# A hybrid decoder layer on one core: the memory projection moved to the front, and the first two column tiles made an ordinary pair

## The chip, the cores and the metric

One core of a Trainium2 chip runs the whole program in one launch. The metric is device time in microseconds (us). The engines are TensorE (PE, with its weight loads as PEld), VectorE (DVE), ScalarE (ACT), GpSimd (POOL) and SyncE (SP), which issues the transfers between the chip's memory and the core.

## The reference, cut to what matters

One layer over 1,056 tokens (1,024 of a prompt and 32 of decoding) with 2,048 features, all in float32. Only group D, the memory attention, and the projections are touched by the change.

```
h    = rmsnorm(x, g_norm)                       # x: 1056 x 2048
proj = h @ w_in                                 # columns of groups A (conv), B (GLA), C (window), D (memory)
kv   = rmsnorm(mem, g_mem) @ w_mem_kv           # mem: 256 x 2048, kv: 256 x 1024
k, v = split(kv);  k = rmsnorm(k per head, g_mem_k)
q    = rmsnorm(m_q per head, g_mem_q)           # 4 heads of 128
o    = softmax(q k^T / sqrt(128)) v;  y_d = o * silu(m_z)
y    = x + concat(y_a, y_b, y_c, y_d) @ w_out
```

## The kernel before

Everything lies transposed: features on the partitions, tokens along the row. Each float32 operand of a large product is split into a rounded high part and the remainder (names ending in h and l), and three products (wh sh, wl sh, wh sl) stand for one.

**Pairs.** The projections go by pairs of column tiles (128 columns each), as a Strassen product with seven products per pair and phase. A phase is one half of the 2,048 features. `first_pair` runs the first half and keeps the sums in memory (`half_in`), `second_pair` adds the second half. One product (`product`, L668) is 24 matmuls of 128 x 264. The seven combinations of x (B11, T2, B21, T1, T3, B22, T4) stay in the on-chip memory for a whole phase. `make_weights` makes the weight side of a product (ACT rounds, L644; DVE takes the remainder, L645, and makes sums, L626 to L640). `ORDER` names the pairs: 22 of the input projection. The first phase runs all 22, then the second phase all 22 with the attention and the other groups beside them, then eight output pairs go through both phases.

**Start.** The tiles Dq0 and Dq1 (the queries of heads 0 and 1) are no pair. `first_two` multiplies them by x directly (L406, 288 matmuls of 128 x 352, both halves of the features), while `load_x` brings x tile by tile (k = 0 to 15), splits it (ACT L310, DVE L311), squares it (ACT L289) and adds the squares up (DVE L294). `row_norms` makes R, the scale of each token, along every partition. The result is scaled on its way out of PSUM (L415) to two tiles dq, which are held until their attention is done.

**First strands.** `first_strands` is a generator. It scales the first half of x by g_norm and R (L444, `normal`), makes the seven combinations (L470 to L482), splits each (`split`, ACT L429, DVE L430) and computes a small product for group B, `rank` (L498). `product` advances it when a combination is missing.

**Memory.** `memory` is a generator too: 16 steps, one per 128 features of the memory tokens, each with 12 matmuls of 128 x 512 (L902). It scales and splits the memory tokens (`prepare`, ACT L848, DVE L849), splits the weights (`weights`, ACT L881, DVE L882) and sums squares as a tree (`squares`, ACT L856, DVE L858). It advances with the strands inside the first pair. `memory_out` scales the keys and values.

**Heads.** `d_head` queues the attention of one head: a preparation and four units of 256 tokens (`d_unit`, L1007 scores, L1029 transposes, L1037 values). A pipe (`_Pipe`) starts queued work at two steps per product. Heads 0 and 1 are queued after the first pair of the first phase. Heads 2 and 3 follow the pair Dq2, Dq3 of the second phase, and behind them `d_decode` (its key and value loads kc and vc). A gate of group D then waits for it.

A scheduler places the instructions of each engine before the run; on an engine they run in that order. All transfers are issued by SP, in order, with eight semaphores in rotation: a load waits for the one eight before it. The pool `rt` has ten buffers of a full row of tokens (x tiles, squares, d, q, z, kc, vc), the pool `sp` fourteen of 2,112 columns.

Of the kernel before, what the change touches and what calls it, by code (L numbers as in the profile page):

```python
# [14 lines left out]
P = 128  # L15
# [6 lines left out]
NCH = 3  # L22
# [100 lines left out]
class _Step:  # L123
    def __init__(self, nc, tc, ctx, I, O):
# [19 lines left out]
        self.pieces, self.raw, self.ready, self.done = [], [], [], 0  # L144
        self.xh, self.xl = [None] * KT, [None] * KT
# [127 lines left out]
    def load_x(self):  # L273


        nc = self.nc
        self.acc = [None] * 2
        last = None
# [5 lines left out]
        self.x0, self.x0raw = block, raw  # L284

        def square(k, parts):
            sq = self.rtile("sq") if k < 8 else parts[2]
            for i, p in enumerate(parts[:2]):
                nc.scalar.activation(sq[:, i * H : i * H + H], p, AF.Square)  # L289
            i = int(k % 4 == 3)  # L290
            if self.acc[i] is None:
                self.acc[i] = sq
            else:
                nc.vector.tensor_tensor(self.acc[i], self.acc[i], sq, op=ALU.add)  # L294
        for k in range(KT):
            if k < 8:
                parts = [block(2 * (k // 4) + i, k % 4) for i in range(2)]
            else:
                xr = self.rtile("xr")
                parts = [xr[:, 0:H], xr[:, H:TOK], xr]  # L300
            if k < 8:
                for i in range(2):
                    nc.sync.dma_start(out=parts[i], in_=self.I["xT"][k, :, i * H : i * H + H])
            else:
                nc.sync.dma_start(out=parts[2], in_=self.I["xT"][k])
            hl = self.stile(F32R, "xhl")
            for i in range(2):
                h, l = (hl[:, x * TOK + i * H : x * TOK + i * H + H] for x in range(2))
                g = self.gn[:, k : k + 1]
                nc.scalar.activation(h, parts[i], AF.Copy, scale=g)  # L310
                nc.vector.scalar_tensor_tensor(l, parts[i], g, h.bitcast(F32), op0=ALU.mult,  # L311
                                               op1=ALU.subtract)
            self.xh[k], self.xl[k] = hl[:, 0:TOK], hl[:, TOK : 2 * TOK]
            if last:
                square(*last)
            last = k, parts
            if k == KT - 1:
                square(*last)
            yield k

    def row_norms(self, spare):

        nc = self.nc
        acc = self.acc[0]
        nc.vector.tensor_tensor(acc, acc, self.acc[1], op=ALU.add)
        for sums in self.token_sums(acc[:, 0:SEQ]):
            pass
        nc.tensor.matmul(spare[:, 0:2], acc[:, TOK - P : TOK], self.ones[:, 0:2], start=True,
                         stop=True)
        r = self.small(NB + 1, tag="rx")  # L330
        self.rsqrt(r[:, 0:NB], sums, 1.0 / D_MODEL, EPS, NB)
        self.rsqrt(r[:, NB : NB + 1], spare[:, 0:1], 1.0 / D_MODEL, EPS, 1)
        for g in range(3):
            ps = self.ps() if g == 1 else spare
            blocks = list(range(4 * g, min(4 * g + 4, NB + 1)))
            for i, n in enumerate(blocks):
                nc.tensor.transpose(ps[:, i * P : i * P + P],
                                    r[:, n : n + 1].to_broadcast([P, P]), self.ident)
            if g < 2:
                nc.scalar.copy(self.R[:, 512 * g : 512 * g + 512], ps)  # L340
            else:
                nc.scalar.copy(self.R[:, SEQ:TOK], ps[:, P - NS : P])

    def load_piece(self):
        kind, src = self.pieces[len(self.raw)]
        wr = self.wp.tile([P, 512], F32, name=self.name("wr"), tag="wr", bufs=6)
        self.nc.sync.dma_start(out=wr, in_=src)
        self.raw.append(wr)  # L350

    def split_piece(self):
        nc = self.nc
        n = len(self.ready)
        wr = self.raw[n]

        if n % 2:
            wh, wl = self.r5(), self.r5()
        else:
            wh, wl = self.weights()  # L360
        if n:
            nc.scalar.copy(wh, wr)
        else:
            nc.vector.tensor_copy(wh, wr)
        eng = nc.gpsimd if 0 < n < 8 else nc.vector
        eng.tensor_tensor(wl, wr, wh.bitcast(F32), op=ALU.subtract)
        self.ready.append((wh, wl))
# [4 lines left out]
    def take(self, ahead=2):  # L372
        p = self.done
        self.done += 1
        last = len(self.pieces) - 1
        while len(self.ready) <= min(p + ahead, last):
            while len(self.raw) <= min(len(self.ready) + 1, last):
                self.load_piece()
            self.split_piece()
        while len(self.raw) <= min(p + ahead + 1, last):  # L380
            self.load_piece()
        return self.ready[p]

    def first_two(self, evacs):

        nc = self.nc
        a, b = self.two(), self.two()
        ps = [[a[:, 0:512], a[:, 512:1024], b[:, 0:512]], [self.ps() for _ in range(NCH)]]
        self.load_piece()
        xs = self.load_x()  # L390
        next(xs)
        self.load_piece()
        for _ in range(3):
            next(xs)
        for kq in range(4):
            w = [self.take(1) for _ in range(2)]
            for kk in range(4):
                next(xs, None)
                k = 4 * kq + kk
                for i in range(2):  # L400
                    wh, wl = w[i]
                    ks = slice(kk * P, kk * P + P)
                    pairs = [(wh, self.xh[k]), (wl, self.xh[k]), (wh, self.xl[k])]
                    for c in range(NCH):
                        for n, (y, x) in enumerate(pairs):
                            nc.tensor.matmul(ps[i][c][:, 0:CW], y[:, ks],  # L406
                                             x[:, c * CW : c * CW + CW], start=(k == 0 and n == 0),
                                             stop=(k == KT - 1 and n == 2))
                if kq == 3 and kk == 1:
                    self.row_norms(b[:, 512:1024])  # L410
        for i in range(2):
            dst = evacs[i]
            for c in range(NCH):
                cs = slice(c * CW, c * CW + CW)
                nc.vector.tensor_tensor(dst[:, cs], ps[i][c][:, 0:CW], self.R[:, cs], op=ALU.mult)  # L415
# [16 lines left out]
    def first_strands(self):  # L432
# [7 lines left out]
        def normal(b):  # L440
            for k in range(4 * (b // 2), 4 * (b // 2) + 4):
                x = self.x0(b, k % 4)
                h = slice(H * (b % 2), H * (b % 2) + H)
                v.scalar_tensor_tensor(x, x, self.gn[:, k : k + 1], self.R[:, h], op0=ALU.mult,  # L444
                                       op1=ALU.mult)
# [6 lines left out]
        ps = self.two()  # L452
# [378 lines left out]

    def memory(self, pool):
# [6 lines left out]
        raw = [None] * KT  # L839
        parts = {}  # L840

        def prepare(k):
            mh, ml = self.r5(), self.r5()
            for i in range(2):
                m = raw[k // 8][:, (k % 8 + i) * N_MEM : (k % 8 + i + 1) * N_MEM]
# [7 lines left out]
        def squares(k):  # L853
            nonlocal acc
            t = raw[k][:, 0 : 8 * N_MEM]
# [8 lines left out]
        for k in range(2):  # L864
            raw[k] = self.stile(F32, "mr")
            nc.sync.dma_start(out=raw[k][:, 0 : 8 * N_MEM].rearrange("p (k t) -> p k t", k=8),
                              in_=I["memT"][8 * k : 8 * k + 8].rearrange("k p t -> p k t"))
        wraw, ready = {}, {}

        def load(k):  # L870
            if k < KT:
                wraw[k] = self.rtile("wm")
                nc.sync.dma_start(out=wraw[k][:, 0:1024], in_=I["w_mem"][k])

        def weights(k):
            w = wraw.pop(k)
            ready[k] = []
            for c in range(2):
                wh, wl = self.weights() if c else [self.t5().bitcast(F32R) for _ in range(2)]
                x = w[:, 512 * c : 512 * c + 512]  # L880
                nc.scalar.copy(wh, x)  # L881
                nc.vector.tensor_tensor(wl, x, wh.bitcast(F32), op=ALU.subtract)  # L882
                ready[k].append((wh, wl))
            load(k + 2)
# [1055 lines left out]
```

## Time and profile before

| | |
|---|---|
| time, median of 3 runs | 1568.07 us (1562.56 to 1576.54) |
| the profiled execution | 1575.27 us, span 1573.5 us |
| PE, PEld, DVE, ACT busy | 97%, 93%, 70%, 49% of the span |
| chain that ended last | PE 75%, DVE 13%, ACT 5%, DMA 4% |
| HBM read, written | 165.38 MB, 69.41 MB |

Times below are from the start of the span. A row of a group reads: line, engine, operation, out<-in, shapes, count | busy us, mean ns of one | idle time of the engine just before, and what ended it. A row of the timeline reads: start, length, engine, line, operation, count [idle before <- what ended it]. An xN on a timeline row is the number of records; a matmul on plain float32 leaves two records.

### The profile page before, as it was taken

What the parts mean: (1) busy time and instruction counts of PE and PEld (TensorE: products, weight loads), DVE (VectorE), ACT (ScalarE), POOL (GpSimd) and SP (SyncE); (2) the same over time, 40 slices, a digit from 0 to 9 for tenths busy, and PEclk for the clock granted to TensorE, in tenths of its full rate; (3) what the DMA queues carried; (4) which work ended last, traced back from release to release, by engine and by line L of the source; (5) the groups of instructions that cost most, each with busy time, mean ns of one, the idle gap of its engine ahead of it and who ended that gap; (6) DMA issues with size and microseconds to landing.
All of it is one profiled execution on the core that took longest, in us unless ns stands there. A gap on an engine that the chain in (4) does not pass through costs nothing.

```text
span 1573.5 us, 30753 instructions
## 1 busy us (share of the span) xinstructions
PE 1530.4 (97%) x12194; PEld 1459.6 (93%) x12194; DVE 1105.2 (70%) x2283; ACT 772.6 (49%) x1620; POOL 23.3 (1%) x35
## 2 busy tenths in 40 slices
PE   7889999999999999999999999999998999999998
PEld 7668999999999999988998999999988999999998
DVE  8998645586555559665767776967779777596664
ACT  8466633322333336744468774645557443363332
POOL 3000000000000000000000000000000000000000
PEclk9899999999999999999999999999999999999999
DMA  7523222375332248158423333533437224587651
GB/s 272 193 92 109 69 103 94 142 267 193 109 110 100 95 148 308 62 144 298 139 78 84 109 90 121 173 123 90 167 119 244 82 104 168 188 288 267 209 203 63
DMA packets 102418, 236.77 MB, mean 150 GB/s; under 512 B 16516, under 2 KB 22532, under 8 KB 102276
## 3 DMA queue, kind: packets, MB, share of 16 engines
q1 hardware_dynamic: 102276, 234.82, 44.4%
q8 instruction: 96, 1.57, 0.4%
q14 instruction: 46, 0.38, 0.1%
HBM read 165.38 MB, written 69.41 MB: 149 GB/s over the span
## 4 chain that ended last, share of the span: by engine, by line
PE 75%; DVE 13%; ACT 5%; DMA 4%; issue 3%; SPq 0%; DVEq 0%; ACTq 0%
PE pj L668 64%; PE ms L902 2%; DVE wl L645 2%; DMA sx<-xs 1%; DVE s L430 1%; DVE xhl L311 1%; ACT wh L644 1%; ACT t L1280 1%; PE ms L1037 1%; DMA x<-in_xT 1%; ACT xhl L310 1%; DMA kc<-in_cache_mem_kT 1%; DVE t L1267 1%; PE ms L1313 1%; PE ms L1007 1%
## 5 line engine op out<-in xcount | busy, mean ns | idle before, releaser
L668 PE MATMUL pj<-s,wh 128*128 128x264 f32 x6720 | 1268.7, 288 | 7.6 <-ACT pj L751 5.5
L668 PEld LDWEIGHTS pj<-s,wh 128*128 128x128 f32 x6720 | 1055.5, 189 | 25.6 <-issue 12.7
L668 PE MATMUL pj<-s,wl 128*128 128x264 f32 x3360 | 960.3, 286 | 0.8 <-DVE wl L645 0.8
L668 PEld LDWEIGHTS pj<-s,wl 128*128 128x128 f32 x3360 | 636.7, 190 | 5.9 <-issue 4.1
L644 ACT CAST wh<-wr 128x512 fp32r<-128x512 f32 x300 | 186.3, 621 | 262.4 <-PE pj L668 248.3
L645 DVE TENSOR_TENSOR wl<-wr,wh 128x512 fp32r<-128x512 f32 x300 | 206.5, 688 | 119.8 <-ACT wh L644 119.4
L698 DVE TENSOR_TENSOR d<-d,pj 128x528 f32<-128x528 f32 x180 | 121.4, 701 | 102.1 <-PE pj L668 60.0
L644 ACT CAST wh<-ws 128x512 fp32r<-128x512 f32 x120 | 74.5, 621 | 93.9 <-PE pj L668 89.5
L645 DVE TENSOR_TENSOR wl<-ws,wh 128x512 fp32r<-128x512 f32 x120 | 82.5, 688 | 9.1 <-ACT wh L644 8.5
L751 ACT COPY pj<-d 128x528 f32<-128x528 f32 x120 | 72.5, 604 | 15.1 <-DVE u L761 5.5
L430 DVE TENSOR_TENSOR s<-sx,s 128x1056 fp32r<-128x1056 f32 x42 | 51.6, 1250 | 1.9 <-ACT s L429 1.9
L429 ACT CAST s<-sx 128x1056 fp32r<-128x1056 f32 x42 | 44.3, 1075 | 10.0 <-DMA sx<-xs 5.2
L772 DVE TENSOR_TENSOR d<-d,pj 128x528 f32<-128x528 f32 x30 | 21.1, 703 | 36.5 <-PE pj L668 36.5
L701 ACT COPY d<-pj 128x528 f32<-128x528 f32 x30 | 18.0, 599 | 55.1 <-PE pj L668 55.1
L707 ACT COPY d<-pj 128x528 f32<-128x528 f32 x30 | 18.0, 601 | 53.4 <-PE pj L668 53.4
L1280 ACT ACTIVATE t<-t,sm,sm 128x256 f32<-128x256 f32 (+1 forms) x64 | 37.1, 581 | 14.2 <-DVE sm L1272 14.2
L640 DVE TENSOR_TENSOR wr<-wr,ws 128x512 f32<-128x512 f32 x60 | 41.8, 697 | 1.0
L775 DVE TENSOR_TENSOR d<-u,pj 128x528 f32<-128x528 f32 x30 | 21.1, 703 | 30.1 <-PE pj L668 30.0
L626 DVE TENSOR_TENSOR ws<-wr,wr 128x512 f32<-128x512 f32 x60 | 41.3, 688 | 1.2
L636 DVE TENSOR_TENSOR wr<-wr,wr 128x512 f32<-128x512 f32 x60 | 41.3, 688 | 1.1
L627 DVE TENSOR_TENSOR ws<-ws,wr 128x512 f32<-128x512 f32 x60 | 41.3, 688 | 1.0
L778 DVE TENSOR_TENSOR d<-u,pj 128x528 f32<-128x528 f32 x30 | 21.1, 703 | 29.8 <-PE pj L668 29.6
(368 smaller groups left out, 1524.2 us busy)
## 6 DMA issues: line engine op xcount, KB each, us to landing
wr<-in_w_in SPq DMA_DIRECT2D x184, 256.0 KB
half_in<-d SPq DMA_DIRECT2D x44, 528.0 KB
d<-half_in SPq DMA_DIRECT2D x44, 528.0 KB
sx<-xs SPq DMA_DIRECT2D x42, 528.0 KB
wr<-in_w_out SPq DMA_DIRECT2D x64, 256.0 KB
x<-in_xT SPq DMA_DIRECT2D x24, 528.0 KB
xs<-t SPq DMA_DIRECT2D x36, 264.0 KB
half_out<-d SPq DMA_DIRECT2D x16, 528.0 KB
```

The lines of the kernel that those rows point to most:

```text
L429: nc.scalar.copy(h[:, s], x)
L430: nc.vector.tensor_tensor(l[:, s], x, h[:, s].bitcast(F32), op=ALU.subtract)
L626: v.tensor_tensor(s1, r(1, 0), r(1, 1), op=ALU.add)
L627: v.tensor_tensor(s2, s1, r(0, 0), op=ALU.subtract)
L636: v.tensor_tensor(x, r(0, 0), x, op=ALU.subtract)
L640: v.tensor_tensor(x, x, self.wsum[n][1], op=ALU.subtract)
L644: nc.scalar.copy(wh, x)
L645: v.tensor_tensor(wl, x, wh.bitcast(F32), op=ALU.subtract)
L668: nc.tensor.matmul(ps[:, 512 * c : 512 * c + CG], w[:, ks], x[:, xs], start=(first and kk == 0 and n == 0), stop=(kk == 3 and n == 2), ski ...
L698: nc.vector.tensor_tensor(o, o, bank(ps), op=op)
L751: nc.scalar.copy(bank(ps), x)
L1280: nc.scalar.activation(ps[u][:, g, kts[0] : 2], ps[u][:, g, kts[0] : 2], AF.Exp, bias=mx[:, c : c + 1], scale=rq[:, 4 * m + c : 4 * m + c ...
```

## The change

1. `first_two`, `load_x` with its split of x, and the weight pieces for it are gone. Dq0 and Dq1 stand at the head of `ORDER`, so there are 23 pairs in each phase of the input projection.
2. A new `start` brings x (`load_x(k)`), the memory tokens (`load_mem`) and w_mem (`load_mem_weights`) interleaved. It advances `memory` by 8 steps, and by 3 more inside `row_norms`. ACT squares x. DVE multiplies the first eight tiles of x by g_norm in place. PE sums the squares over the partitions (`sum_squares`: four matmuls of 32 x 264 for each k, at four column positions of the array, into one bank of PSUM).
3. `normal` multiplies a block by R alone: one operation on 2,112 columns, or two on 1,056.
4. `memory` splits 1,024 columns of a weight tile in one operation of each engine, into a buffer of the pool `sp`.
5. All four heads are queued in the second phase, each two behind their pair.

```
+    def square(self, k):
+        nc = self.nc
+        if k < 8:
+            sq = self.sq[k] = self.rtile("sq")
+            for i in range(2):
+                x = self.x0(2 * (k // 4) + i, k % 4)
+                nc.scalar.activation(sq[:, i * H : i * H + H], x, AF.Square)
+                nc.vector.tensor_scalar(x, x, self.gn[:, k : k + 1], None, op0=ALU.mult)
+        else:
+            nc.scalar.activation(self.sq[k], self.sq[k], AF.Square)
+    def sum_squares(self, k):
+        for j in range(4):
+            self.nc.tensor.matmul(self.sums[32 * j : 32 * j + 32, 0:CG], self.ones[:, 0:32],
+                                  self.sq[k][:, CG * j : CG * j + CG], start=(k == 0),
+                                  stop=(k == KT - 1), tile_position=(0, 32 * j))
...
+        def loads(k):
+            if k in (1, 4, 7):
+                self.load_mem(k // 3 + 1)
+            if k + 2 < KT:
+                self.load_mem_weights(k + 2)
+            for i in range(2):
+                if 2 * k + i < KT:
+                    self.load_x(2 * k + i)
+        for k in range(2):
+            loads(k)
+        for k in range(8):
+            if k + 2 < 8:
+                loads(k + 2)
+            next(self.mem)
+            for i in range(2):
+                self.square(2 * k + i)
+            if k:
                 for i in range(2):
+                    self.sum_squares(2 * k - 2 + i)
+        self.load_weights(0, ((0, 0), (1, 0), (1, 1), (0, 1)))
+        self.make_weights()
         for i in range(2):
+            self.sum_squares(KT - 2 + i)
+        for _ in self.row_norms(spare):
+            next(self.mem)
...
         def normal(b):
-            for k in range(4 * (b // 2), 4 * (b // 2) + 4):
-                x = self.x0(b, k % 4)
-                h = slice(H * (b % 2), H * (b % 2) + H)
-                v.scalar_tensor_tensor(x, x, self.gn[:, k : k + 1], self.R[:, h], op0=ALU.mult,
-                                       op1=ALU.mult)
+            r = self.R[:, H * (b % 2) : H * (b % 2) + H].unsqueeze(1)
+            for x in self.x0raw[b] if b == 3 else [self.x0raw[b]]:
+                n = x.shape[1] // H
+                t = x.rearrange("p (k t) -> p k t", k=n)
+                v.tensor_tensor(t, t, r.to_broadcast([P, n, H]), op=ALU.mult)
...
-    ORDER = ["Dq2", "Dq3", "Ac0", "Ah0", "Az0", "Ab0", "Dz0", "Dz1", "Dz2", "Dz3",
+    ORDER = ["Dq0", "Dq1", "Dq2", "Dq3", "Ac0", "Ah0", "Az0", "Ab0", "Dz0", "Dz1", "Dz2", "Dz3",
...
                     if n == 0:
                         self.masks()
-                        for h in range(2):
-                            self.d_head(q[h], h)
                 pipe.drain()
                 done = [2]
-                self.second(hold(q))
-                for h in (2, 3):
-                    self.d_head(q[h], h)
+                for i in (0, 2):
+                    self.second(hold(q))
+                    for h in (i, i + 1):
+                        self.d_head(q[h], h)
```

Three places show how instructions move. The first is ACT in the changed kernel, some twenty operations into the program. Names: r is a scaled part of the memory tokens, wm the high half of a weight tile of memory, sq a tile of squares of x, xr an x tile of the second half that is squared in place (xr_240 is k = 8, sq_303 and sq_308 are k = 6 and 7).

```order
L827 ACTIVATE r_244<-mr_129,consts 128x256 x2
L850 CAST wm_250<-wr_134 128x1024
L850 CAST wm_288<-wr_146 128x1024
L297 ACTIVATE sq_265<-xb_125 128x528
L297 ACTIVATE sq_265<-xb_126 128x528
L297 ACTIVATE sq_270<-xb_125 128x528
L297 ACTIVATE sq_270<-xb_126 128x528
L300 ACTIVATE xr_240<-xr_240 128x1056
L827 ACTIVATE r_327<-mr_129,consts 128x256 x2
L300 ACTIVATE xr_242<-xr_242 128x1056
L297 ACTIVATE sq_303<-xb_125 128x528
L297 ACTIVATE sq_303<-xb_127 128x528
```

The square of k = 8 stands ahead of those of k = 6 and 7, though SP loads it behind them.

The second place is DVE where the first block of x is scaled by R; before the change it stood like this (dq: the direct product's result, xb_128: the first block of x, t and wl: low halves of memory's weights).

```order
L415 TENSOR_TENSOR dq_120<-ms_125,R_118 128x352
L444 SCALAR_TENSOR_TENSOR xb_128<-xb_128,consts,R_118 128x528 x4
L882 TENSOR_TENSOR t_747<-wm_736,t_746 128x512
L882 TENSOR_TENSOR wl_751<-wm_736,wh_750 128x512
L444 SCALAR_TENSOR_TENSOR xb_129<-xb_129,consts,R_118 128x528 x2
L430 TENSOR_TENSOR s_785<-xb_128,s_784 128x2112
L882 TENSOR_TENSOR t_763<-wm_738,t_762 128x512
```

In the changed kernel DVE has at the same place (sm: the small steps of the inverse root, mr: the tree of memory's squares, L410: the scaling, L395: the low half of a combination):

```order
L268 SCALAR_TENSOR_TENSOR sm_508<-sm_527,sm_508 8x4
L828 SCALAR_TENSOR_TENSOR r_622<-mr_236,consts,r_621 128x256 x2
L591 TENSOR_TENSOR ws_1110<-wr_466,wr_1007 128x512
L601 TENSOR_TENSOR wr_466<-wr_464,wr_466 128x512
L837 TENSOR_TENSOR mr_236<-mr_236 128x1024
L410 TENSOR_TENSOR xb_123<-xb_123,R_118 128x2112
L410 TENSOR_TENSOR xb_124<-xb_124,R_118 128x2112
L395 TENSOR_TENSOR s_618<-xb_123,s_617 128x2112
L851 TENSOR_TENSOR wm_627<-wr_432,wm_627 128x1024
L851 TENSOR_TENSOR wm_676<-wr_544,wm_676 128x1024
```

Thirteen of memory's sixteen weight tiles are split by then where none was, and the tree's first addition (L837) stands right ahead of the scaling.

The third place is PE in the changed kernel at the end of the start (pj_128 holds the sums of squares, then the transposes; ms_154 to ms_157 are memory's sums of which the first is shown).

```order
L306 MATMUL pj_128<-xr_360,ones 32x264 x4
L306 MATMUL pj_128<-xr_362,ones 32x264 x4
L873 MATMUL ms_154<-wm_429,r_391 128x512 x2
L873 MATMUL ms_154<-wm_429,r_392 128x512
L873 MATMUL ms_156<-wm_429,r_391 128x512 x2
L873 MATMUL ms_156<-wm_429,r_392 128x512
L873 MATMUL ms_155<-wm_429,r_391 128x512 x2
L873 MATMUL ms_155<-wm_429,r_392 128x512
L873 MATMUL ms_157<-wm_429,r_391 128x512 x2
L873 MATMUL ms_157<-wm_429,r_392 128x512
L320 MATMUL pj_128<-ident,t_480 128x128 x2
L322 MATMUL pj_128<-ident,t_480 8x128
```

One step of the memory product stands between the last sum of squares and the transposes of the sums.

More of the change, by code (lines that the diff above doesn't have):

```diff
@@ L295, in load_x @@
[L295 to L306, printed above, removed]
-            for i in range(2):
[L308 to L319, printed above, removed]
+        self.x0, self.x0raw, self.sq = block, raw, [None] * KT
@@ L326, in row_norms @@
[L326 to L342, printed above, removed]
@@ L346, in load_piece @@
[L346 to L367, printed above, removed]
+        rows = self.t5()[:, 0:CG]
@@ L369, in weights @@
+        yield
     def weights(self):
         return [self.wp.tile([P, 512], F32R, name=self.name(x), tag=x) for x in ("wh", "wl")]
[L372 to L399, printed above, removed]
-                for i in range(2):
[L401 to L410, printed above, removed]
+    def start(self, pool):
+        self.x_tiles()
+        self.mem_tiles = {}
+        self.mem = self.memory(pool)
+        bank = self.two()
+        self.sums, spare = bank[:, 0:512], bank[:, 512:1024]
+        self.spare = spare
+        self.load_mem(0)
+        for k in range(2):
+            self.load_mem_weights(k)
+        def loads(k):
[6 more added lines that the diff above has]
+                    self.load_x(2 * k + i)
+        for k in range(2):
+            loads(k)
[6 more added lines that the diff above has]
+            if k:
+                for i in range(2):
+                    self.sum_squares(2 * k - 2 + i)
+        self.load_weights(0, ((0, 0), (1, 0), (1, 1), (0, 1)))
+        self.make_weights()
@@ L863, in squares @@
                 nc.vector.tensor_copy(acc, t[:, 0:N_MEM])
[L864 to L873, printed above, removed]
-        def weights(k):
[L876 to L884, printed above, removed]
-        load(0)
-        load(1)
+        ready = {}
+        def weights(k):
+            t = self.mem_tiles["w", k // 2]
+            x = t[:, 1024 * (k % 2) : 1024 * (k % 2) + 1024]
+            hl = self.stile(F32R, "wm")
+            wh, wl = hl[:, 0:1024], hl[:, 1024:2048]
+            nc.scalar.copy(wh, x)
+            nc.vector.tensor_tensor(wl, x, wh.bitcast(F32), op=ALU.subtract)
+            ready[k] = [(wh[:, 512 * c : 512 * c + 512], wl[:, 512 * c : 512 * c + 512])
+                        for c in range(2)]
+            if k % 2:
+                del self.mem_tiles["w", k // 2]
+            if k >= 6 and k + 4 < KT:
+                self.load_mem_weights(k + 4)
         prepare(0)
```

81 lines of the change are left out of this document (49 added, 32 removed).

## The prediction

> **What bounds the kernel now.** I read the page first (span, engines, slices), then busy time by stage, then single rows of the early stages.
>
> ```profile
> span 1573.5 us, 30753 instructions
> PE 1530.4 (97%) x12194; PEld 1459.6 (93%) x12194; DVE 1105.2 (70%) x2283; ACT 772.6 (49%) x1620; POOL 23.3 (1%) x35
> ...
> DVE  8998645586555559665767776967779777596664
> ...
> 0.00:66.00 66.00, 54.18 (x311) 50.83 (x312) 56.64 (x97) 49.17 (x87) 15.29 (x18) 0.97 0.74 257
> 66.00:154.40 88.40, 81.53 (x467) 66.61 (x466) 81.34 (x134) 53.76 (x93) 1.08 (x5) 0.91 0.30 99
> 154.40:215.40 61.00, 60.28 (x446) 56.27 (x447) 37.05 (x106) 37.05 (x92) 0.00 (x0) 1.00 0.23 81
> 215.40:317.70 102.30, 102.26 (x844) 101.92 (x847) 58.82 (x88) 31.72 (x56) 0.00 (x0) 1.00 0.34 121
> 615.30:735.80 120.50, 116.05 (x983) 104.90 (x982) 71.73 (x153) 64.22 (x156) 3.95 (x9) 0.99 0.53 166
> ```
>
> The columns of the stages are length, PE, PEld, DVE, ACT, POOL, granted clock, DMA share, GB/s. PE carries the kernel, but not at its start: in the first slices DVE is at 8 or 9 tenths, and from 66 to 154 us it is busy 81.3 of 88.4 us, with the clock down to 0.91. From 215 to 318 us PE is busy without a gap. So work that leaves DVE counts before 154 us; later only PE's work counts.
>
> The beats of the program are the first eviction of each pair (L701 in the first phase, L757 in the second):
>
> ```profile
> 154.38 0.60 ACT L701 COPY d<-pj 128x528 f32<-128x528 f32 x1
> ...
> 215.42 0.60 ACT L701 COPY d<-pj 128x528 f32<-128x528 f32 x1 [2.29 <-PE pj L668]
> ...
> 296.99 0.60 ACT L701 COPY d<-pj 128x528 f32<-128x528 f32 x1 [2.30 <-PE pj L668]
> ...
> 615.25 0.59 ACT L757 COPY u<-pj 128x528 f32<-128x528 f32 x1
> ...
> 735.81 0.60 ACT L757 COPY u<-pj 128x528 f32<-128x528 f32 x1 [0.92 <-PE pj L668]
> ```
>
> Four undisturbed pairs take 296.99 - 215.42 = 81.6 us, 20.4 us for a pair in a phase. The two pairs from 154.38 take 61.0 us: heads 0 and 1 beside them cost 61.0 - 40.8 = 20.2 us, and PE is busy 60.3 of it.
>
> **The sum in outline.** Take the first eviction of the *second* pair: 154.4 us before, Y in the change. Behind it the change has one more pair in the first phase and one more in the second (22 and 23 pairs where there were 21 and 22). So the time moves by (Y - 154.4) + 2 x 20.4, and by what the moved heads cost more or less.
>
> **Up to R.** The scale R is needed for the first product. Before, the first block is scaled at 66.5 us. What leaves DVE ahead of that are the low halves of x and the sums of squares:
>
> ```profile
> L311 DVE SCALAR_TENSOR_TENSOR xhl<-xr,consts,xhl 128x528 fp32r<-128x528 f32 x16 | 15.5, 1013 | 0.0
> L311 DVE SCALAR_TENSOR_TENSOR xhl<-xb,consts,xhl 128x528 fp32r<-128x528 f32 x16 | 13.0, 857 | 1.7 <-ACT xhl L310 1.7
> L294 DVE TENSOR_TENSOR sq<-sq,xr 128x1056 f32<-128x1056 f32 x8 | 9.9, 1244 | 0.0
> L294 DVE TENSOR_TENSOR sq<-sq,sq 128x1056 f32<-128x1056 f32 x6 | 8.3, 1385 | 0.2 <-ACT sq L289 0.2
> ...
> L1444 DVE TENSOR_SCALAR la<-la 128x528 f32<-128x528 f32 x2 | 0.9, 428 | 0.0
> ```
>
> That is 46.7 of 56.6 us. New are 16 scalings by g_norm of 528 columns; the trace's one group of that form takes 0.43 us, so 7 us, covered by the loads. It does not bring R forward by as much, since loads and ACT take DVE's place:
>
> ```profile
> 0.00:8.00 8.00, 1.17 (x3) 0.80 (x4) 2.75 (x13) 3.85 (x9) 1.07 (x10) 1.00 0.67 204
> 8.00:24.00 16.00, 15.97 (x92) 15.51 (x92) 15.09 (x17) 16.00 (x28) 4.29 (x3) 1.00 1.04 391
> ...
> L289 ACT ACTIVATE xr<-xr 128x528 f32<-128x528 f32 x16 | 10.3, 646 | 2.8 <-DVE xhl L311 2.6
> L962 ACT ACTIVATE sq<-dq 128x1024 f32<-128x1024 f32 x1 | 1.1, 1056 | 0.0
> L848 ACT ACTIVATE r<-mr,consts 128x256 fp32r<-128x256 f32 x10 | 4.7, 504 | 4.3 <-PE ms L902 4.2
> L856 ACT ACTIVATE mr<-mr 128x2048 f32<-128x2048 f32 x2 | 3.8, 1915 | 0.0
> ```
>
> Through the last x tile SP now issues 16 x tiles of 0.54 MB, ten of w_mem and four of memT of 0.52 MB each: 16.2 MB with the constants. The queue moves 204 x 8 = 1.6 MB in the first 8 us and 391 GB/s when full: 8 + 14.6/0.391 = **45 us**. ACT's order is the harder limit. It squares x's ninth tile ahead of the seventh, and 10.3 MB lie up to that tile: 8 + 8.7/0.391 = 30 us. Until then the squares of x 6 and 7 and the casts behind them wait, though their data are there. From 30 ACT has eight squares of 1056 columns, four of 528, four casts of 1024, four scalings and the tree's square: 8 x 1.1 + 4 x 0.6 + 4 x 1.06 + 4 x 0.5 + 1.9 = 19 us, 18 since neighbours overlap a little. So the last square ends near 48, its sum on PE near **50 us**.
>
> From there the order names what stands between: one k of the memory product on PE, the transposes, two chains of 13 small DVE operations with ten larger ones among them, transposes, copies.
>
> ```profile
> 85.59 1.67 PE L902 MATMUL ms<-t,r 128*128 128x512 f32 x6
> ...
> 88.49 1.55 PE L902 MATMUL ms<-t,r 128*128 128x512 f32 x6
> ...
> 58.38 0.16 DVE L264 TENSOR_SCALAR sm<-sm 128x8 int32<-128x8 int32 x1
> ...
> 59.59 0.26 DVE L270 SCALAR_TENSOR_TENSOR sm<-sm,sm 128x8 f32<-128x8 f32 x2
> ...
> L882 DVE TENSOR_TENSOR t<-wm,t 128x512 fp32r<-128x512 f32 x16 | 10.9, 683 | 0.0
> L858 DVE TENSOR_TENSOR mr<-mr 128x1024 f32<-128x1024 f32 x2 | 2.4, 1218 | 0.0
> ```
>
> A k of memory is 88.49 - 85.59 = 2.9 us, so the transposes start at 53. Interleaved small operations run at 0.09 us (14 from 58.38 to 59.59), those of 512 columns at 0.6. The chains with their company take 26 x 0.09 + 6 x 0.6 + 2 x 0.4 + 2 x 1.15 = 9 us: 62. The first pair's weight tiles, now behind memory's on SP's queue, land at 50 to 54 and are just in time. Then come transposes, and on ACT the memory square (1.9) between the copies of R; DVE's first addition of the tree (1.2) waits for that square and stands ahead of the first scaling: **66 us**. R is a wash. Bounds: 58 if ACT keeps up with the loads (45 + 13), 76 if PE is late too (below).
>
> **From R to Y** DVE stays the bound, and loses what went ahead of R:
>
> ```profile
> L882 DVE TENSOR_TENSOR wl<-wm,wh 128x512 fp32r<-128x512 f32 x16 | 10.9, 683 | 0.3 <-ACT wh L881 0.3
> L849 DVE SCALAR_TENSOR_TENSOR r<-mr,consts,r 128x256 fp32r<-128x256 f32 x12 | 5.2, 477 | 0.0
> L444 DVE SCALAR_TENSOR_TENSOR xb<-xb,consts,R 128x528 f32<-128x528 f32 x16 | 11.4, 761 | 0.0
> L430 DVE TENSOR_TENSOR s<-xb,s 128x2112 fp32r<-128x2112 f32 x4 | 9.4, 2350 | 0.0
> ```
>
> Of 21.8 us of memory's low halves three k of 1.2 us are left: -18. The scaled memory tiles go (-5), most of the tree of squares (-3), the scaling becomes four passes of 2112 columns (9.4 for 11.4: -2), the eviction of the old pair (-1). That makes 29 of 88 us; splits, combinations, weights and evictions stay. Y = 66 + 59.5 = **125.5 us**. Bounds: 118 and 134 for this stage's 5 us of waits either way on top of R's.
>
> PE is no bound here. The 64 small products of the squares resemble the rank products:
>
> ```profile
> 93.82 0.40 PE L902 MATMUL ms<-wh,r 128*128 128x512 f32 x1
> 94.15 1.97 PE L498 MATMUL pj<-xb,t 128*16 128x264 f32 x32
> 96.05 1.20 PE L902 MATMUL ms<-t,r 128*128 128x512 f32 x4
> ```
>
> 32 records of the same 264 columns take 1.9 us, so 128 take 7.6. Memory (16 x 2.9), these, ranks (4) and eight products of 2.9 make 81 us of 125. The Trainium skill, TensorEngine Tiling (Key Properties), speaks against this mixture: a change of the tiling mode drains TensorE, and the change makes some 17 of them. The trace bears it out only just: 93.82 to 94.15 is 0.33 us where memory's products follow at 0.24, so 0.1 us each, 2 us in all by that rule, on an engine with slack.
>
> **The heads.** Heads 0 and 1 leave the first phase (-20.2). In the second, the four pairs from 615.25 take 120.5, 38.9 over 4 x 20.4, with PE busy 116.05: heads 2, 3 and the decode there are PE time too. So two more cost 20 us again, hidden by nothing. Bounds: -2 (some of the 4.5 us of idle PE there is filled) to +8 (the decode's cache loads come late behind SP's base loads). I take +0.5, nearer to PE's row. Queues: SP's loads of the second pass of x find two buffers more free; at nothing.
>
> **Sum.** 125.5 - 154.4 = -29; two phases of a pair +40.8; heads +0.5: **+12 us**. The profiled execution took 1575.3 us (span 1573.5), so 1587 there; it lies 7 us over the median of 1568.1, and on that scale it is **1580 us**.
>
> **Rivals.**
> *The old start was the dearer one (not slower).* If ACT does not wait for the ninth tile and the last square follows the loads, R is at 58, and Y at 117: 12 - 8 = +4; with the stage behind also 5 us shorter, -1: 1567 to 1572. It needs R by 58; for 1% faster R would have to come at 38, when 2.7 MB of the loads are still out. For it: ACT's sum to the last square is only 35 us. Against: the order, and the tree's square right in R's way.
>
> *PE at half clock.*
>
> ```profile
> 60.00:64.00 4.00, 2.41 (x11) 1.88 (x12) 2.40 (x11) 1.45 (x4) 0.00 (x0) 0.71 0.89 314
> 64.00:68.00 4.00, 3.43 (x10) 2.27 (x8) 3.04 (x7) 0.95 (x2) 0.00 (x0) 0.50 0.95 387
> ...
> 69.95 2.07 PE L902 MATMUL ms<-t,r 128*128 128x512 f32 x4 [2.52 <-DVE t L882]
> ```
>
> After gaps of 2 to 2.5 us the clock stood at 0.50. In the change PE waits for ACT round by round. If it falls to half and stays, a round of memory and two sums costs 2 x (2.9 + 1) = 7.8 us, eight of them 62 where I have 41: R at 76 to 87, +10 to +21, **1590 to 1601**. Against: a round at half clock leaves no gaps, so the clock should return. The Trainium skill, TensorE: Matmul & The Clock Gate (What's actually happening), gives windows of about 3.4 us, idle to fall and busy to rise; by that rule PE's longest gap, five us before the ninth tile lands, costs one slow window, 2 us.
>
> *The second phase stalls.* Sixteen units now run through three pairs, and the decode through two more, with four q tiles, two z and two base tiles held. If each vc load waits for a buffer behind PE, eight waits of 1 us: +8, 1588.
>
> **How the numbers follow.** Forecast (8 to 16 us slower) 0.45; near to even 0.2; half clock 0.2; second phase late 0.1; something else, faster, 0.05. The range takes in the bounds 58 and 76 of R and half of the stalls: 1563 to 1600. A change within 1% (15.7 us) is about what a measurement of this kernel can't tell from none; my forecast lies just inside, so slower by over 1% gets the half clock, the stalls and a part of the forecast's spread.
>
> **What would show it.** First scaling (the R multiplication, DVE) at 66; eviction of the second pair at 125; pairs behind at 20.4 us, from the third on with no heads; three second-phase pairs at 33 to 35 us. Clock in 20 to 60 us under 0.8 means the half clock. I am wrong if R is off by over 10 us or if a pair beside the heads takes over 36 us.

## The result and the profile after

The change made the kernel 1% slower: 1584.72 us median of six runs against 1569.13 before (six), ratio 1.0101 (95% interval 1.0069 to 1.0133). A second set of runs of both gave 1582.89 against 1570.59, ratio 1.0077 (1.0058 to 1.0096). That is +12 to +16 us, where the forecast was +12.

The page after begins like this; the rows answer to those of before:

```profile
span 1580.0 us, 30999 instructions
PE 1529.1 (97%) x12364; PEld 1451.2 (92%) x12364; DVE 1082.4 (69%) x2250; ACT 758.4 (48%) x1582; POOL 9.6 (1%) x28
...
DVE  4886556765555586555767776867879767586664
```

DVE is no longer at 8 or 9 tenths in the first slices, and PE's total is what it was (1529.1 us against 1530.4). The stages of the changed kernel (length, PE, PEld, DVE, ACT, POOL, clock, DMA share, GB/s):

```profile
0.00:68.60 68.60, 53.33 (x296) 35.28 (x296) 41.82 (x95) 45.01 (x67) 1.26 (x11) 0.95 0.83 311
68.60:128.90 60.30, 46.13 (x309) 37.27 (x310) 55.47 (x89) 30.21 (x53) 1.14 (x5) 0.83 0.12 39
128.90:169.70 40.80, 40.80 (x338) 40.80 (x337) 22.93 (x36) 12.69 (x23) 0.00 (x0) 1.00 0.33 118
588.10:767.10 179.00, 175.16 (x1436) 160.58 (x1435) 110.71 (x249) 105.70 (x255) 4.14 (x9) 1.00 0.45 146
```

And the beats, the first eviction of the second pair and of two pairs of the second phase (that of the fourth pair stands at 169.68):

```profile
128.90 0.60 ACT L666 COPY d<-pj 128x528 f32<-128x528 f32 x1 [2.20 <-PE pj L633]
...
588.13 0.60 ACT L722 COPY u<-pj 128x528 f32<-128x528 f32 x1
...
767.09 0.60 ACT L722 COPY u<-pj 128x528 f32<-128x528 f32 x1 [0.55 <-PE pj L633]
```

The second pair's eviction came 25.5 us earlier (154.4 to 128.9). The next two pairs take 40.8 us where they took 61.0 beside heads 0 and 1. In the second phase, the stretch that ends behind all heads takes 179.0 us where it took 140.95 with one pair less (the beats of before, 615.25 to 756.2).

The way to R in the changed kernel (ACT's squares, PE's last sums and first transposes, DVE's tree and first scaling):

```profile
31.52 1.08 ACT L300 ACTIVATE xr<-xr 128x1056 f32<-128x1056 f32 x1 [7.92 <-DMA xr<-in_xT]
...
47.23 2.06 ACT L300 ACTIVATE xr<-xr 128x1056 f32<-128x1056 f32 x2
...
51.16 1.10 PE L306 MATMUL pj<-xr,ones 128*32 128x264 f32 x16
...
55.09 0.38 PE L320 MATMUL pj<-ident,t 128*128 128x128 f32 x2
...
67.44 1.23 DVE L837 TENSOR_TENSOR mr<-mr 128x1024 f32<-128x1024 f32 x1 [0.71 <-ACT mr L835]
68.58 4.62 DVE L410 TENSOR_TENSOR xb<-xb,R 128x2112 f32<-128x2112 f32 x2
```

ACT waits 7.9 us for x's ninth tile, the last square ends at 49.3, and the tree's addition stands right ahead of the first scaling at 68.6.

### The profile page after: what moved, and what is told of

Read it like the earlier page. It is cut to its first block, busy times and chain, and to the rows that moved or that the text cites. A ratio compares the mean times of both kernels' runs of the same rounds, so it can differ in the third digit from the quotient of the medians.

```text
span 1580.0 us, 30999 instructions
## 1 busy us (share of the span) xinstructions
PE 1529.1 (97%) x12364; PEld 1451.2 (92%) x12364; DVE 1082.4 (69%) x2250; ACT 758.4 (48%) x1582; POOL 9.6 (1%) x28
## 4 chain that ended last, share of the span: by engine, by line
PE 79%; DVE 10%; ACT 5%; DMA 4%; issue 2%; SPq 0%; ACTq 0%; DVEq 0%
PE pj L633 67%; PE ms L873 2%; DVE wl L610 2%; DMA xb<-in_xT 1%; DVE s L395 1%; DMA x<-in_xT 1%; PE ms L978 1%; ACT wh L609 1%; ACT t L1251 1%; PE ms L1008 1%; DMA out_conv_s<-sm 1%; DVE t L1238 1%; PE ms L1284 1%; DMA wr<-in_w_mem 1%; PE ms L1272 1%
## 5 line engine op out<-in xcount | busy, mean ns | idle before, releaser
L633 PE MATMUL pj<-s,wh 128*128 128x264 f32 x6944 | 1308.8, 287 | 17.5 <-ACT s L394 9.0
L633 PEld LDWEIGHTS pj<-s,wh 128*128 128x128 f32 x6944 | 1087.3, 189 | 38.0 <-issue 13.5
L633 PE MATMUL pj<-s,wl 128*128 128x264 f32 x3472 | 990.0, 285 | 0.1
L633 PEld LDWEIGHTS pj<-s,wl 128*128 128x128 f32 x3472 | 656.6, 189 | 3.7 <-issue 2.9
L609 ACT CAST wh<-wr 128x512 fp32r<-128x512 f32 x310 | 192.5, 621 | 267.5 <-PE pj L633 254.6
L610 DVE TENSOR_TENSOR wl<-wr,wh 128x512 fp32r<-128x512 f32 x310 | 213.3, 688 | 128.8 <-ACT wh L609 128.4
L663 DVE TENSOR_TENSOR d<-d,pj 128x528 f32<-128x528 f32 x186 | 125.5, 701 | 108.9 <-PE pj L633 59.8
L873 PE MATMUL ms<-wm,r 128*128 128x512 f32 x192 | 52.4, 423 | 8.6 <-ACT wm L850 8.6
L873 PEld LDWEIGHTS ms<-wm,r 128*128 128x128 f32 x192 | 37.0, 200 | 22.0 <-ACT wm L850 10.7
L395 DVE TENSOR_TENSOR s<-sx,s 128x1056 fp32r<-128x1056 f32 x42 | 51.6, 1251 | 0.9 <-ACT s L394 0.9
L740 DVE TENSOR_TENSOR d<-u,pj 128x528 f32<-128x528 f32 x31 | 21.8, 703 | 32.3 <-PE pj L633 32.2
```

What stands on the lines that cost most here:

```text
L395: nc.vector.tensor_tensor(l[:, s], x, h[:, s].bitcast(F32), op=ALU.subtract)
L610: v.tensor_tensor(wl, x, wh.bitcast(F32), op=ALU.subtract)
L633: nc.tensor.matmul(ps[:, 512 * c : 512 * c + CG], w[:, ks], x[:, xs], start=(first and kk == 0 and n == 0), stop=(kk == 3 and n == 2), ski ...
L663: nc.vector.tensor_tensor(o, o, bank(ps), op=op)
L873: nc.tensor.matmul(ps[t][c], a[:, ts], b, start=(k == 0 and i == 0), stop=(k == KT - 1 and i == 2))
```

## The experiments

Ratios are to the kernel before, timed in turn with it on the same chip. "Y" is the eviction of the second pair as in the prediction.

| kernel | ratio (95%) | first scaling | Y |
|---|---|---|---|
| the change | 1.0101 (1.0069 to 1.0133) | 68.6 | 128.9 |
| the change, again | 1.0077 (1.0058 to 1.0096) | 67.7 | 127.2 |
| before, again | 0.9995 (0.9984 to 1.0006) | 66.5 | 152.8 |
| heads_late | 0.9961 (0.9943 to 0.9978) | 66.8 | 152.7 |
| old_start_pe_sums | 1.0049 (1.0035 to 1.0063) | 72.3 | 160.5 |
| mem_in_pair | 1.0057 (1.0041 to 1.0073) | 38.0 | 124.8 |
| squares_apart | 1.0075 (1.0051 to 1.0099) | 67.1 | 127.0 |
| new_start_dve_sums | 1.0110 (1.0087 to 1.0134) | 73.5 | 134.3 |
| less_dve (leaves work out) | 1.0049 (1.0031 to 1.0067) | 62.8 | 121.4 |
| norms_alone | 1.0055 (1.0040 to 1.0070) | 59.4 | 120.5 |
| heads_late_no_pool | 0.9950 (0.9934 to 0.9965) | 62.6 | 148.9 |

### Both kernels once more

> The changed kernel once more, unchanged. In the first pair of profiles the change cost 6.8 us, by the medians 15.6. Theory (the sum of the early terms is right, +11 us at 767 us of the span, and the rest is scatter of single executions at the places that wait for transfers): again a first scaling at 68 to 69, the second pair's eviction at 128 to 130, and 10 to 14 us over the kernel before by the medians. Rival (a term of the changed kernel differs from one execution to the next): eviction or second-phase pairs off by over 2 us.

> The kernel before once more. Theory (its first profile, 1575.3 us, was one of its slower executions, by waits for transfers behind 950 us): second pair's eviction within 2 us of 154.4, second phase from 615 to 756 within 1 us, and the difference to the first profile behind it. Rival (the start scatters): eviction at 150 to 152.

The beats of the second profiles, before and then the change (timeline of ACT):

```profile
152.82 0.60 ACT L701 COPY d<-pj 128x528 f32<-128x528 f32 x1
...
612.05 0.59 ACT L757 COPY u<-pj 128x528 f32<-128x528 f32 x1
...
752.00 0.60 ACT L757 COPY u<-pj 128x528 f32<-128x528 f32 x1 [0.55 <-PE pj L668]
```

```profile
127.16 0.60 ACT L666 COPY d<-pj 128x528 f32<-128x528 f32 x1 [2.20 <-PE pj L633]
...
589.50 0.59 ACT L722 COPY u<-pj 128x528 f32<-128x528 f32 x1
...
768.74 0.60 ACT L722 COPY u<-pj 128x528 f32<-128x528 f32 x1 [0.55 <-PE pj L633]
```

The early terms repeat within 2 us: Y moves by 25.7 us (25.5 in the first pair of profiles), and the second-phase stretch is 139.95 and 179.24 us (140.95 and 178.96). The two spans of the change are 1580.0 and 1583.5, those of before 1573.5 and 1565.9. So the profiles differ by 6.5 us in one pair and by 17.6 in the other, 12 on average, as the medians do. Between Y and the second phase one kernel alone differs by 1.6 us (before) and 3.1 us (the change) from one profile to the other. So one pair of profiles shows which stages changed, not the size of a 1% change.

### The heads alone

```
-                        for h in range(2):
-                            self.d_head(q[h], h)          # behind the first pair of phase 1
...
+                for h in range(2):
+                    self.d_head(q[h], h)                  # ahead of the first pair of phase 2
                 self.second(hold(q))
```

> The kernel before with only part 5 of the change: heads 0 and 1 are queued in front of the first pair of the second phase. By the traces of before and after, two heads cost 20.2 us in the first phase and 17.6 in the second. Theory (heads are TensorE time wherever they stand, with a small gain in the second phase's gaps): 2 to 3 us faster than before; the three first-phase pairs behind the first at 20.4 us each, some five pairs of the second phase at 17 to 18 us more. Rival (the decode's transfers come late behind the added units): one pair of the second phase over 37 us, 3 to 8 us slower than before.

The beats of heads_late:

```profile
152.70 0.60 ACT L701 COPY d<-pj 128x528 f32<-128x528 f32 x1
...
593.06 0.59 ACT L757 COPY u<-pj 128x528 f32<-128x528 f32 x1
...
749.67 0.60 ACT L757 COPY u<-pj 128x528 f32<-128x528 f32 x1 [0.55 <-PE pj L668]
```

From Y to the second phase it takes 440.4 us where the second profile of before took 459.2 (-18.9). The stretch behind takes 156.6 where it took 139.95 (+16.7). That is -2 us; against the first profile of before it is -5. The time fell by 0.39%, 6 us (3.5 to 9). So this part of the change is a gain, more than the 2 to 3 us that I had expected. The rival did not show: the first two pairs of the second phase take 35.0 and 35.1 us here (beats 593.06, 628.02, 663.09), the next three less, and it asked for one over 37.

### The squares on TensorE, in the old start and out of the new one

The first kernel is before, with `sum_squares` and the new `row_norms` in its start:

```
-                nc.vector.tensor_tensor(self.acc[i], self.acc[i], sq, op=ALU.add)
+            for j in range(4):
+                nc.tensor.matmul(self.sums[32 * j : 32 * j + 32, 0:CG], self.ones[:, 0:32],
+                                 sq[:, CG * j : CG * j + CG], start=(k == 0),
+                                 stop=(k == KT - 1), tile_position=(0, 32 * j))
```

> The kernel before with one part of the change alone: x's squares are summed on TensorE (64 matmuls of 32 x 264) and not on DVE; the direct product, memory and the heads stay. Theory (DVE carries the start): 18 us of sums and 1.2 of the closing one leave DVE ahead of R; the first scaling comes at 56 to 60 instead of 66.5, the second pair's eviction 6 to 10 us earlier than 154.4, 6 to 10 us faster than before. Rival (TensorE is as full: 54 of 66 us, and takes 8 us of sums and 16 changes of its tiling more): first scaling at 65 to 70, within 3 us of before or slower.

The rival held in its direction, and by more than it said. The stage from 48 to 66 us of this kernel, then its first scaling and its Y:

```profile
48.00:66.00 18.00, 18.00 (x129) 15.87 (x128) 1.86 (x3) 0.91 (x2) 0.43 (x1) 1.00 0.57 185
```

```profile
72.29 1.45 DVE L447 SCALAR_TENSOR_TENSOR xb<-xb,consts,R 128x528 f32<-128x528 f32 x2 [1.53 <-ACT R L344]
...
160.50 0.61 ACT L704 COPY d<-pj 128x528 f32<-128x528 f32 x1
```

DVE is busy for 1.9 of 18 us, PE has no gap, and R is 5.8 us later (72.3, where the rival had 65 to 70): in the old start the direct product filled TensorE as the splits filled DVE. Taking load off one of two full engines by putting it on the other cost 0.5%.

The second kernel is the change with the sums back on DVE:

```
+        if k:
+            nc.vector.tensor_tensor(self.acc, self.acc, self.sq[k], op=ALU.add)
```

> The changed kernel with the squares of x added up on DVE (15 additions of 1056 columns, 17.6 us) instead of the 64 small matmuls, which is the other half of the test of summing on TensorE. From 8 to 48 us DVE has 17.4 us free. Theory (in the new start TensorE has room and DVE too, both in the loads' shadow; only the last additions stand behind the last square): first scaling at 69 to 72, eviction of the second pair at 129 to 133, 0 to 4 us slower than the changed kernel. Rival (the 64 matmuls hold up memory's products on TensorE, as they held up the direct product in the old start): first scaling and eviction earlier than 68.6 and 128.9, by 2 us or more.

R came at 73.5 and Y at 134.3, both beyond the theory's upper ends. By the ratios it was 5 us slower than the change in the same rounds (1.0110 against 1.0077), but the two intervals overlap: its six times lie from 1582.6 to 1592.5 us, two of them at the change's, and the profile is of the longest. In that profile the cause stands on DVE: its last addition, in turn with memory's work, ends at 56 us, where PE's last sum of the change ends at 52.

```profile
54.89 1.25 DVE L302 TENSOR_TENSOR sq<-sq,xr 128x1056 f32<-128x1056 f32 x1
```

So summing on TensorE cost 8 us in the old start, where TensorE had no room. In the new one it is worth some 5 us by the trace, and the times alone do not show it.

### ACT's order or the loads

```
-            sq = self.sq[k] = self.rtile("sq")
+            if k % 2 == 0:
+                self.sq2 = self.stile(F32, "sq")
+            sq = self.sq[k] = self.sq2[:, TOK * (k % 2) : TOK * (k % 2) + TOK]
```

> The changed kernel, the squares of x tiles 0 to 7 in buffers of the pool sp, so that on ACT the squares of k = 6 and 7 stand ahead of that of k = 8. Theory of the prediction (ACT's order sets the last square): ACT's 7.9 us of idle before 31.5 us are filled, the last square ends near 43 to 45, the first scaling comes 4 to 6 us earlier (63 to 65), the eviction of the second pair at 123 to 125, 4 to 6 us faster than the changed kernel. Rival (the loads set it: the queue is full to 48 us whatever ACT does, and the last x tiles land at about 46): last square at 47 to 49, first scaling at 67 to 69, within 2 us of the changed kernel.

The timeline of ACT and DVE in squares_apart:

```profile
31.55 1.08 ACT L302 ACTIVATE xr<-xr 128x1056 f32<-128x1056 f32 x1 [4.09 <-DMA xr<-in_xT]
...
45.62 2.06 ACT L302 ACTIVATE xr<-xr 128x1056 f32<-128x1056 f32 x2
...
67.14 2.35 DVE L412 TENSOR_TENSOR xb<-xb,R 128x2112 f32<-128x2112 f32 x1
```

ACT's wait halves to 4.1 us, but the ninth tile lands when it did, and the last square ends at 47.7 instead of 49.3 (48.7 in the second profile). R gains 0.5 to 1.4 us. The rival's numbers held, its reason only in part: behind the tenth tile ACT waits for no load any more. Four squares of 528 columns and two scalings, 3.1 us, are now done ahead of the ninth tile, and of that 1.6 us came out, since ACT now stands 1.4 us for PE's memory step. So the loads set the start of ACT's last stretch, ACT's own work its length, and the order was worth under 2 us.

### Memory back in the first pair

```
-            next(self.mem)
...
-        for _ in self.row_norms(spare):
-            next(self.mem)
+        for _ in self.row_norms(spare):
+            pass
```

Also, x is loaded first, and `memory` with its own loads is that of the kernel before.

> The changed kernel with the memory projection in its old place and its old form (inside the first pair, 512 columns at a time); x is loaded first, and its squares are still summed on TensorE. Theory (up to the second pair's eviction it is the sum of DVE's work that counts, not where it stands): the first scaling at 42 to 48 instead of 68.6, but about 26 us of memory's low halves, scalings and tree come behind it, so that the second pair's first eviction stands at 125 to 133 (changed kernel 128.9), time within 4 us of the changed kernel. Rival (R sets the rest of the start, the memory work fits into gaps): eviction at 105 to 110, 20 us faster than the changed kernel and faster than before.

The first scaling and Y of mem_in_pair, and its stage up to Y:

```profile
38.04 2.36 DVE L394 TENSOR_TENSOR xb<-xb,R 128x2112 f32<-128x2112 f32 x1 [2.33 <-ACT R L336]
...
124.83 0.60 ACT L650 COPY d<-pj 128x528 f32<-128x528 f32 x1
```

```profile
54.80:124.80 70.00, 66.84 (x410) 54.86 (x408) 66.04 (x108) 46.15 (x82) 1.08 (x5) 1.00 0.26 83
```

R came 30 us earlier, and Y only 2 to 4: the stretch between them is 86.8 us, 26.5 longer. That is nearly what was expected (R came 4 us before the range, Y at its early end), but the stage row says more than my theory: PE is as full there as DVE (66.8 and 66.0 of 70 us), so this run does not tell which of the two sets it. Memory's move to the front gains nothing by itself; this kernel was no slower than the change (1.0057 against 1.0077 and 1.0101).

### From R to the second pair: DVE's sum, or the chain

```
-            nc.vector.tensor_tensor(wl, x, wh.bitcast(F32), op=ALU.subtract)
+            if k < 11:
+                nc.vector.tensor_tensor(wl, x, wh.bitcast(F32), op=ALU.subtract)
+            else:
+                wl = wh
...
+            if k:
+                return                      # no second tree
```

> The changed kernel, from which work of DVE is left out that the first pair's chain of scaling, combinations, splits and products does not need: the low halves of w_mem from k = 11 on (five of 1.17 us; the high half is multiplied twice, TensorE's work stays) and the second tree of memory's squares (2.7 us). Some 6.2 us of it stand at or behind the first scaling, 2.3 ahead of it. Theory (DVE's sum of work sets the stretch from R to the second pair): first scaling 2 to 4 us earlier, the second pair's eviction 6 to 9 us earlier (120 to 123). Rival (the chain of dependent operations and waits sets it): eviction 0 to 3 us earlier.

```
-        for _ in self.row_norms(spare):
-            next(self.mem)
+        for _ in self.row_norms(spare):
+            pass
```

> The kernel squares_apart, in which memory makes no steps beside the row norms: its last eight steps all run inside the first pair. Ahead of the first scaling DVE loses two low halves of w_mem (2.3 us) and the first addition of the second tree with the wait for ACT's square (1.9 us), TensorE up to three steps of memory (8.7 us); all of it comes behind. Theory A (behind R, DVE has gaps: with 5 us less work there the stretch from R shrank by only 1 to 2 us): first scaling at 61 to 63, stretch from R to the second pair 60 to 62, eviction at 121 to 125, 5 to 8 us faster than the changed kernel, still 4 to 8 us slower than before. Theory B (the sum of DVE's work counts): first scaling at 61 to 63, stretch 64 to 66, eviction at 126 to 129, as in the changed kernel.

First scaling and Y of less_dve, then of norms_alone:

```profile
62.83 2.36 DVE L410 TENSOR_TENSOR xb<-xb,R 128x2112 f32<-128x2112 f32 x1 [0.44 <-ACT R L336]
...
121.38 0.60 ACT L666 COPY d<-pj 128x528 f32<-128x528 f32 x1 [2.21 <-PE pj L633]
```

```profile
59.42 2.35 DVE L412 TENSOR_TENSOR xb<-xb,R 128x2112 f32<-128x2112 f32 x1
...
120.50 0.60 ACT L668 COPY d<-pj 128x528 f32<-128x528 f32 x1 [2.30 <-PE pj L635]
```

less_dve hit the forecast for Y, but not by its theory. R was 5 to 6 us earlier, more than expected, and the stretch behind it shrank from 60.3 (59.5 in the second profile) to 58.6 us only. norms_alone did the opposite: three steps of memory and DVE's work for them went behind R, and the stretch grew to 61.1 only, as theory A had it; R, at 59.4, was earlier than both theories said. The stages from R to Y, less_dve and then norms_alone:

```profile
62.80:121.40 58.60, 47.15 (x332) 39.81 (x331) 52.83 (x86) 33.08 (x56) 1.14 (x5) 0.88 0.12 40
```

```profile
59.40:120.50 61.10, 53.32 (x340) 42.84 (x341) 57.82 (x88) 34.88 (x56) 0.20 (x1) 0.89 0.14 50
```

DVE is busy there for 52.8, 55.5 (the change) and 57.8 us. It changes by less than the work left out or moved, since with R earlier some of the work on weights falls behind it. Over these 5.0 us the stretch moves by 2.5: at most about half of DVE's work counts there, and the rest fits into gaps (norms_alone also has some 8 us more of PE's work there than squares_apart). What stands beside the row norms delays R: moving it away, 4.2 us of DVE's time and up to 8.7 of PE's, brought R from 67.1 (squares_apart) to 59.4. The time is 3 us under that of squares_apart and 3 to 7 under the change by the ratios (1.0055), with intervals that overlap in part, and it is still above before.

### GpSimd off the old start

```
-        eng = nc.gpsimd if 0 < n < 8 else nc.vector
+        eng = nc.vector
```

> The kernel heads_late with the seven splits of the direct product's weights moved from GpSimd to DVE. In the trace of before DVE's operations on 528 columns take 0.72 us while GpSimd rests (35 to 48 us) and 1.48 us while it works (28.8 to 34.7 us). Theory (GpSimd costs DVE as much as it takes off it): DVE gains 5 to 6 us of slowed operations and gets 4.8 us of splits; first scaling within 1.5 us of 66.8, time within 3 us of heads_late, 4 to 9 us faster than before. Rival (TensorE's waits for GpSimd, 2.1 us, go as well): first scaling at 62 to 65, eviction of the second pair at 148 to 151, 8 to 11 us faster than before. Rival (the moved splits stand in DVE's way, where it was full): first scaling at 69 to 72, no faster than before.

In the first profile of before, DVE's split of x beside GpSimd and without it, and the last of four operations of GpSimd in a row from 25.3 us on:

```profile
28.84 5.91 DVE L311 SCALAR_TENSOR_TENSOR xhl<-xr,consts,xhl 128x528 fp32r<-128x528 f32 x4
...
35.84 1.43 DVE L311 SCALAR_TENSOR_TENSOR xhl<-xr,consts,xhl 128x528 fp32r<-128x528 f32 x2
```

```profile
31.75 1.76 POOL L366 TENSOR_TENSOR wl<-wr,wh 128x512 fp32r<-128x512 f32 x1
```

The first row mixes two kinds: three of its four operations took 1.79 us each, and the fourth, which starts at 34.0 when GpSimd has ended (33.5), took 0.76. So the 1.48 us of the expectation is their mean, and the slowing is larger than it says.

In heads_late_no_pool the same groups (busy, mean ns of one), its first scaling and its Y:

```profile
L311 DVE SCALAR_TENSOR_TENSOR xhl<-xb,consts,xhl 128x528 fp32r<-128x528 f32 x16 | 11.6, 766 | 1.1 <-ACT xhl L310 1.1
L311 DVE SCALAR_TENSOR_TENSOR xhl<-xr,consts,xhl 128x528 fp32r<-128x528 f32 x16 | 11.5, 772 | 0.0
```

```profile
62.64 2.12 DVE L444 SCALAR_TENSOR_TENSOR xb<-xb,consts,R 128x528 f32<-128x528 f32 x3
...
148.90 0.60 ACT L701 COPY d<-pj 128x528 f32<-128x528 f32 x1
```

The split of x takes 23.1 us of DVE instead of 28.5, more than the 4.9 us that the seven splits add. R is 4.1 us and Y 3.8 us earlier than in heads_late, where the first rival had them, but not by its reason: PE still waits 1.3 us for these splits, now on DVE, where heads_late waited 1.8 for GpSimd. Ahead of R, DVE's busy time fell from 57.1 to 55.2 us and its idle time from 9.6 to 7.4; which waits went, and why, was not tried. With 0.9950 this is the fastest version here, 8 us under before and 20 to 24 under the change; its distance to heads_late (0.9961) is within both intervals, and rests on the trace.

## Why the prediction was right, and where not

**The sum.** Forecast: -29 by Y, +40.8 by two phases of a pair, +0.5 by the heads, +12. By the two pairs of profiles: -25.6, +40.8, and the heads -20.2 in the first phase and +17.6 or +18.9 in the second, so -2: +13. Measured: +12 to +16. Two terms were off by some 3 us with opposite signs, Y too early and the heads too dear. The mechanism was right, but that the sum came out so close is in part luck. I had also said that a change within 1% is about what a measurement of this kernel can't tell from none; the intervals here reach 0.1 to 0.3% to either side.

**Up to R** I was 2 us early (66, came at 68.6 and 67.7). The ninth tile landed at 31.5 and not at 30, and PE was inside a step of memory when the last square ended at 49.3, so that it began the last sum at 51.2. ACT's work in between was right (17.8 us, 18 in the forecast), and so was the way from the transposes to R (55.1 to 68.6, 13.5 for 13). What failed is a reason: "ACT's order is the harder limit". With that order mended, R moved by 1 us: the ninth tile lands no earlier, and behind it ACT's work and PE's steps take nearly as long as before. I also took the company of the two chains as given (the 9 us, and the tree's addition in front of the scaling), where 8 us of R could be had.

**From R to Y** I said 59.5 and it was 60.3 and 59.5. "DVE stays the bound" held for the large step: DVE's busy time in the stretch fell by 25.9 us (81.3 to 55.5; I had 29) and the stretch by 28. For the next 5 us it held by half, as less_dve and norms_alone show. What sets the rest was not tried. The trace of the change shows a chain there, ACT and then PE:

```profile
98.59 3.81 ACT L394 CAST s<-xb 128x2112 fp32r<-128x2112 f32 x2 [5.76 <-DVE xb L439]
...
100.60 0.59 PE L633 MATMUL pj<-s,wh 128*128 128x264 f32 x1 [7.10 <-ACT s L394]
```

PE waits 9.0 us for ACT's casts of the combinations, 7.1 of them here. The cast waits for DVE's combinations (5.8 us), and the first of these had waited 1.2 us for the ranks on PE, which end at 91.3. From there to the product above it is 9.3 us; in less_dve it is 9.4, though DVE has less to do, and in norms_alone 10.7. With this gap the granted clock fell to 0.50, where it stood from 96 to 108 us. How much of the stretch hangs on this chain no run tells.

**TensorE as no bound** was right for the new start, but for the 1.9 us at the last sum. Its 64 small matmuls cost what I took:

```profile
16.56 1.11 PE L306 MATMUL pj<-sq,ones 128*32 128x264 f32 x16
17.60 3.03 PE L873 MATMUL ms<-wm,r 128*128 128x512 f32 x12
...
46.26 1.99 PE L306 MATMUL pj<-xr,ones 128*32 128x264 f32 x32
48.18 3.05 PE L873 MATMUL ms<-wm,r 128*128 128x512 f32 x12
```

Eight matmuls (16 records) take 1.04 us to the next product's start, sixteen 1.92, so, worked out from these two, 0.11 for each and 0.16 us for a change of the tiling there and back. That is near the 0.1 us for each change that I took for the drain of which the Trainium skill, TensorEngine Tiling (Key Properties), speaks.

**The heads.** I expected no difference (+0.5) and the gap-filling as a bound (-2); it was the bound. The three pairs that I named took 33.9, 35.1 and 33.4 us (beats 610.3, 644.2, 679.3, 712.7), as forecast, and the stalls of the third rival did not come.

**The rivals.** The half clock came, and went again:

```profile
32.00:36.00 4.00, 1.04 (x8) 0.38 (x8) 1.87 (x4) 4.00 (x8) 0.00 (x0) 0.68 1.04 414
36.00:40.00 4.00, 4.00 (x24) 1.79 (x22) 3.35 (x4) 4.00 (x5) 0.00 (x0) 0.50 1.04 389
40.00:44.00 4.00, 4.00 (x25) 2.33 (x26) 1.82 (x3) 3.57 (x5) 0.00 (x0) 0.96 1.04 406
```

After a gap of 6.3 us PE ran at 0.50, and from 40 us on it was back, as I had argued from a round that leaves no gaps. ACT waited 0.4 us for PE behind it, at 42.6; whether PE would have begun the last sum earlier without it, no run tells. The rival of an even result asked for R at 58. norms_alone brought it to 59.4, and Y to 120.5 where the rival had 117, and was still 0.55% slower.

**Where the expected gain went.** From heads_late to mem_in_pair, timed in the same rounds, the direct product is replaced by a pair, with the heads late and memory inside the first pair in both. Y comes 27.9 us earlier, and two phases of a pair cost 40.8 where nothing disturbs them, 13 in all; by the times it is 13 to 15 us (0.9961 against 1.0057). In the two profiles the stretches behind Y, up to the second phase and past the heads, are 21.9 and 22.8 us longer, which is 44.7 and inside their scatter. What the direct product took of TensorE under the loads can be read from the first profile of before:

```profile
40.85 1.62 PE L406 MATMUL ms<-xhl,r 128*128 128x352 f32 x9
42.31 0.32 PE L406 MATMUL pj<-xhl,wh 128*128 128x352 f32 x1
```

Nine matmuls take 1.46 us from start to start, so the 288 some 46 us, an estimate. It cost the path 28; as a pair it costs 40.8 of TensorE where TensorE is full. This swap outweighs what the late heads gain, and makes most of the loss. It is not quite alone in that comparison: in mem_in_pair the squares are also summed on TensorE and x is multiplied by g_norm ahead of R, and the 28 us hold that as well. Memory's move to the front does not bring the loss back: with it the change is another 3 to 7 us slower by the ratios, which the intervals do not settle.

## What to carry to other kernels

Work under the loads at the start is priced by what the start gets shorter without it, not by its own time: a cheaper form of it that runs later, where the main engine is full, can be dearer. When a start has two full engines, moving work from one to the other can make it longer, as it did here by 6 us; look for what stands beside a short chain of dependent steps, such as the row norms, and move that. Try the parts of a change alone: here one of them, the late heads, was a gain that the others hid.

## What the runs showed of the hardware

GpSimd's subtraction of two operands slows DVE beside it: an operation of DVE on 528 columns took 1.79 us against 0.72 to 0.77, and with the seven splits on GpSimd DVE's split of x took 5.4 us more, where doing them itself takes 4.9. The Trainium skill, SBUF — State Buffer (SBUF: two separate sides), says that the two engines share a pair of ports, which one of them holds for a whole instruction, also where DVE reads two inputs; that fits with the direction here, and with its disappearance when GpSimd rests. It fits with the pace too: in the stretch above DVE's operations start at 28.84, 30.56 and 32.27 us and GpSimd's at 30.04 and 31.75, one of each every 1.7 us.
